# Triangle blocks of a gated delta rule solved one block per partition, and no modulation sums during a norm

## The chip, the cores and the metric

The kernel runs on one core of one Trainium2 chip. The metric is the device time of one execution in microseconds (us), lower is better; the time of a kernel is the median of several executions.

## What is computed

One decoder layer with adaLN conditioning: 256 tokens, width 2048, all in float32. A vector `mod` is made from the conditioning vector, then follow a SwiGLU feed-forward (FFN1, inner width 5632), a token mixer with 8 softmax-attention heads and 8 gated-delta-rule heads, a second feed-forward (FFN2) and a last norm.

```python
mod = cond @ ada_w[l] + ada_b[l]
sh1, sc1, gt1, sh2, sc2, gt2, sh3, sc3, gt3 = jnp.split(mod, N_MOD, axis=-1)
h = ada_in(x, norm_g[l, 0], sh1, sc1)          # rmsnorm(x) * (1 + scale) + shift
x = x + MACARON_W * gt1[:, None, :] * swiglu(h, ffn_w_gate[l, 0], ffn_w_up[l, 0], ffn_w_down[l, 0])
h = ada_in(x, norm_g[l, 1], sh2, sc2)
x = x + gt2[:, None, :] * hybrid_mixer(h, w_in[l], w_out[l], ...)
h = ada_in(x, norm_g[l, 2], sh3, sc3)
x = x + MACARON_W * gt3[:, None, :] * swiglu(h, ffn_w_gate[l, 1], ffn_w_up[l, 1], ffn_w_down[l, 1])
return rmsnorm(x, final_norm)
```

Inside the delta rule each head has four chunks of 64 tokens, and for each chunk the inverse of a lower triangle of 64x64 with ones on its diagonal is wanted:

```python
lower = jnp.where(strict, jnp.einsum("bhnid,bhnjd->bhnij", kb, k) * decay, 0.0)
t_inv = lax.linalg.triangular_solve(eye + lower, jnp.broadcast_to(eye, lower.shape),
                                    left_side=True, lower=True, unit_diagonal=True)
u = t_inv @ vb
```

## The kernel before, in words

**The weight stream.** All weights of the two feed-forwards and the mixer pass through one stream of 674 blocks. A block is eight tiles of 128x128. SP issues its load `wraw` (512 KB, L97, three buffers), ScalarE (ACT) casts it to a rounded high part `whi` (L99), VectorE (DVE) subtracts to get the low part `wlo` (L115), and TensorE (PE) multiplies with both parts. A load can only be issued when the `wlo` three blocks earlier is done with its buffer. Blocks 0 to 263 are FFN1, 264 to 377 the projections of the mixer, 378 to 409 its output projection, 410 to 673 FFN2.

**The modulation sums.** `mod` is not made at once: a side job `ada_col` (L237) loads one column group `adat` (1 MB, L256) and lets DVE multiply it with the conditioning and add it up (L258). 140 of these are left for the stream: each block adds a `pace` from the table `RATE` to `W.owed`, and each time that reaches one a sum is put in. While `W.quiet` is set nothing is added. Four finished columns of a gate go through DRAM as a row (`row_send`, gd<-mod, L284; `row_load`, gtr<-gd, L290).

**The norms.** `modulate` (L384) makes the normed and modulated input `hs` in 16 column groups j, of which `h_need` keeps four ahead of the matmuls. For each pair of j: x times the reciprocal norm (`xn`, ACT L401 and DVE L397), transposes on PE into `pxt` (L404), and per j a scale and shift and a split into high and low part (`ht`, `hs`: ACT L409, L410, L412; DVE L413, L414).

**The mixer and its chains.** While the stream's projections run, small serial work of the heads is put between their tiles. Each piece is a Python generator in a chain; `tick` (called per tile, 0.35 us by the kernel's own table) takes the next step of a chain when its due time, the yielded gap times `GAP`, has come. `finish(kind, h)` drains a chain to head h. The order of the projections is a written list, `ORDER = "K3 K4 K5 K6 K7 Z0 G0 V0 F0 G1 ..."`. In the chain "k" lie `gates`, `keys(h)` for each delta-rule head (transposes `pk` L896, products `pkk` L899, and the triangle `Ln` L909), and `solve(half)` behind the keys of heads 3 and 7.

**The solve.** Only the 16x16 blocks on the diagonal of the triangles are inverted here, 64 of them per half (8 matrices of 128 with 8 blocks each). Before, eight transfers bring the blocks of all matrices to DRAM (ld<-Ln, L922), and eight bring them back so that each block's 256 numbers stand on the 16 partitions of its rows (x<-ld, L927). Then 15 steps of a product (L934) and a sum (L935) run on 128 partitions, and L937 spreads the result `U0`, from which `gdn(h)` starts. `solve(0)` stands in "k" ahead of the keys of heads 4 to 7, and step G0 finishes "k".

**Order on an engine.** A scheduler orders the instructions within each engine; an engine runs its list in that order, and an instruction that waits holds all that stand behind it. `tc.issue_after(W.last)` puts a transfer behind the latest weight load in SP's list.

Of the kernel before, what the change touches and what calls it, by code (L numbers as in the profile page):

```python
# [16 lines left out]
P = 128  # L17
# [13 lines left out]
NH = 8  # L31
# [3 lines left out]
N_TILES = 5392  # L35
GR = 24
NEG = -1e30

RATE = ((0, 0.5), (24, 0.34), (56, 0.45), (68, 0.35), (112, 0.45), (168, 0.38), (264, 0.1), (280, 0.18), (408, 0.125))
N_BIG, N_GDN = 3, 3  # L40
# [3 lines left out]
X_LATE = {2: (2, 6), 4: (6, 11), 7: (11, 16)}  # L44
TILE_US = 0.35
MORE = True
GAP = {"k": 1.0, "gdn": 1.0, "fox": 1.2}
ORDER = ("K3 K4 K5 K6 K7 Z0 G0 V0 F0 G1 F1 G2 F2 G3 F3 V1 Z1 G4 F4 G5 F5 G6 F6 G7 F7").split()
N_O = 17
MAGIC = 0x5F3759DF  # L50
# [79 lines left out]
def layer_kernel(ctx: ExitStack, tc: tile.TileContext, xt, xrow, c, adaw, cols, cst, fng, w, out, order, dbg=None):  # L130
# [89 lines left out]
    def C(name, lo_=0, n=None):  # L220
        o, wd = CST[name]
        return cstt[:, o + lo_ : o + (wd if n is None else lo_ + n)]
# [161 lines left out]
    def modulate(which, m_sh, m_sc, hs):  # L384
        ada_need(max(m_sh, m_sc), KD - 1)
        g1 = gains(which, m_sc, 0, KD)
        y = [norm_rstd(t) for t in range(2)]
        st = {}

        def one(j):  # L390

            if j % 2 == 0:
                st["ps"] = psf("pxt")
                for t in range(2):
                    xn = tmp.tile([P, T], F32, name="xn", bufs=4)
                    if t:
                        last = V.tensor_scalar(xn, X(t, j * P, T), y[t], None, ALU.mult)  # L397
                        if j == 0:
                            W.held = [None, sqa["hold"], last.ins]
                    else:  # L400
                        A.activation(xn, X(t, j * P, T), AF.Copy, scale=y[t])  # L401
                    for q in range(2):
                        o = q * T + t * P
                        PE.transpose(st["ps"][:, o : o + P], xn[:, q * P : (q + 1) * P], ident)  # L404
            ps = st["ps"][:, (j % 2) * T : (j % 2 + 1) * T]
            g, sh = g1[:, j : j + 1], mod[:, m_sh * KD + j : m_sh * KD + j + 1]
            t = pt("ht")
            if j % 2:
                A.activation(t, ps, AF.Identity, bias=sh, scale=g)  # L409
                A.copy(hs[:, j, 0], t)  # L410
            else:
                A.activation(hs[:, j, 0], ps, AF.Identity, bias=sh, scale=g)  # L412
                V.tensor_scalar(t, ps, g, sh, ALU.mult, ALU.add)  # L413
            V.tensor_tensor(hs[:, j, 1], t, hs[:, j, 0].bitcast(F32), ALU.subtract)  # L414

        hq["next"], hq["one"] = 0, one

# [12 lines left out]


    clock = {"now": 0.0}
    chains = {"k": [], "gdn": [], "fox": []}
    due = {"k": 0.0, "gdn": 0.0, "fox": 0.0}

    def advance(kind):

# [17 lines left out]
    def start(kind, h, chain):  # L455
        if not chains[kind]:
            due[kind] = clock["now"] + GAP[kind]
        chains[kind].append((h, chain))
# [256 lines left out]
    def mixer():  # L715
# [3 lines left out]
        dram = lambda n, sh: mx.enter_context(tc.tile_pool(name=n + "p", bufs=1, space=bass.MemoryType.DRAM)).tile(sh, F32, name=n)  # L719
        xd = dram("xd", [P, KD, T])  # L720
        rows = dram("rowd", [NH, 2 * T])
        ld = dram("ld", [2 * NH, 8, 16, 16])
        op = mx.enter_context(tc.tile_pool(name="op", bufs=N_O))
        gp = mx.enter_context(tc.tile_pool(name="gp", bufs=1))
        m1p = mx.enter_context(tc.tile_pool(name="m1p", bufs=1))
# [160 lines left out]
        def keys(h):  # L886
# [20 lines left out]
            V.tensor_tensor(nb2, nbt[:, :, h], r2[:, :, h], ALU.mult)  # L907
            for t in range(2):
                V.scalar_tensor_tensor(Ln[:, h, t], pg[:, t * P : (t + 1) * P], nb2[:, t : t + 1], dec[:, t], ALU.mult, ALU.mult)  # L909

        def solve(half):

# [3 lines left out]
            V.tensor_tensor(rb2[:, :, hs4], nbeg[:, :, hs4], r2[:, :, hs4], ALU.mult)  # L916
            rk = rsqrt(ssk[:, :, hs4], [P, 2, 4], "k")
            V.tensor_tensor(rkb[:, :, hs4], rk, colS[:, :, 4, hs4], ALU.mult)
            Lh = Ln[:, hs4].rearrange("p h t j -> p (h t) j")
            for b in range(8):  # L920
                r = slice(16 * b, 16 * b + 16)
                nc.sync.dma_start(ld[ht, b].rearrange("n r c -> r n c"), Lh[r, :, r])  # L922
            rows_ = x[:, ht]
            for b in range(8):
                r = slice(16 * b, 16 * b + 16)
                src = ld[ht, b].rearrange("n r c -> n (r c)").unsqueeze(0).to_broadcast([16, n, 256])
                nc.sync.dma_start(rows_[r], src)  # L927
            yield 9.0
            U = tmp.tile([P, n, 16], F32, name="u16", bufs=1)
            pr = tmp.tile([P, n, 16], F32, name="pr16", bufs=1)  # L930
            G.memset(rows_[:, :, 0:256:17], 1.0)
            V.tensor_copy(U, C("id16").unsqueeze(1).to_broadcast([P, n, 16]))
            for i in range(1, 16):
                V.tensor_tensor(pr[:, :, : i + 1], rows_[:, :, 16 * i : 16 * i + i + 1], U[:, :, : i + 1], ALU.mult)  # L934
                V.tensor_reduce(U[:, :, i], pr[:, :, : i + 1], mybir.AxisListType.X, ALU.add)  # L935
            for q in range(2):
                V.tensor_tensor(  # L937
                    U0[:, hs4].rearrange("p h t (b i) -> p (h t) b i", b=4)[:, 4 * q : 4 * q + 4],
# [200 lines left out]
        def have_keys(h, ps):  # L1139
            kk[h] = otile("kk")  # L1140
            conv_silu(ps, NH + h, kk[h].bitcast(F32)[:, 0])
            start("k", h, keys(h))
            if h % 4 == 3:
                start("k", h, solve(h // 4))

        def step(kind, h):
            if kind == "K":
                have_keys(h, project([("qkv", NH + h)])[0])
            elif kind == "G":
                pq = project([("qkv", h)])[0]  # L1150
                pv = project([("qkv", 2 * NH + h)])[0]
                finish("gdn", h - 3)
                finish("k", h // 4 * 4 + 3)
                qv[h] = otile("qv")
                conv_silu(pq, h, qv[h].bitcast(F32)[:, 0])
                conv_silu(pv, 2 * NH + h, qv[h].bitcast(F32)[:, 1])
# [183 lines left out]
```

## Time and profile before

| | before |
|---|---|
| median of 3 runs | 2103.53 us (2102.01 to 2106.01) |
| the profiled execution's own time | 2100.51 us |
| its span in the trace | 2098.7 us |
| mean granted TensorE clock | 0.983 |
| PE busy | 2010.9 us, 96% of the span |
| DVE busy | 1484.3 us, 71% |
| ACT busy | 991.1 us, 47% |
| DMA traffic | 529.18 MB, 252 GB/s mean |

Durations in the rows are of the one profiled execution. PE is busy almost throughout, so time is lost where PE has a gap, and where the granted clock is below 1.00, since the same matmuls then take longer. A row of the waits names the instruction that was held, what released it, the sum, the number and the longest. A row of the timeline begins with the start and the duration, and ends in brackets with the idle time ahead of it and its releaser. SPq is SP's queue of transfers; a group there lasts from the first issue to the last.

### The profile page before, as it was taken

Reading aid. Unit: us, or ns where it says so; the run is one execution under the profiler, and the core shown is the slowest. Engines: PE = TensorE matmul, PEld = TensorE weight load, DVE = VectorE, ACT = ScalarE, POOL = GpSimd, SP = SyncE. Lnnn points to the kernel's source line nnn. Section 1 sums busy time; section 2 is a strip of 40 time slices with the busy share of each in tenths; the row PEclk is TensorE's granted clock in tenths of the full one; section 3 lists DMA queues with packets and bytes.
Section 4 is the critical chain, followed back from the end, with each engine's and each line's share of the span. In section 5 each row is a group of like instructions: output and inputs, shape, how many; then the busy total and the mean of one; then the engine's idle time right before and its main releaser. Section 6 shows DMA issues by size and latency. Waiting matters only on the chain. (4 is left out here: it accounts for less than half of the span.)

```text
span 2098.7 us, 25397 instructions
## 1 busy us (share of the span) xinstructions
PE 2010.9 (96%) x9347; PEld 1646.8 (78%) x9347; DVE 1484.3 (71%) x2075; ACT 991.1 (47%) x1420; POOL 2.1 (0%) x11
## 2 busy tenths in 40 slices
PE   7899999999999998789999989899999999999998
PEld 4788788777888877667888878778888888888886
DVE  6899888887877867877877876665655554445454
ACT  4544444333434446745756654553444334444443
POOL 0000000000000000000000000000000000000000
PEclk8999999999999999989999999999999999999999
DMA  9899999998888875575556557566776656555553
GB/s 375 313 336 349 337 318 309 375 365 321 335 339 340 324 274 199 160 234 191 183 202 223 195 178 258 198 231 204 274 210 239 205 191 198 191 191 191 203 195 134
DMA packets 138815, 529.18 MB, mean 252 GB/s; under 512 B 23097, under 2 KB 28217, under 8 KB 120385
## 3 DMA queue, kind: packets, MB, share of 16 engines
q1 hardware_dynamic: 138690, 527.56, 70.7%
q8 instruction: 73, 1.20, 0.2%
q14 instruction: 52, 0.43, 0.1%
HBM read 523.13 MB, written 4.37 MB: 251 GB/s over the span
## 5 line engine op out<-in xcount | busy, mean ns | idle before, releaser
L99 ACT CAST whi<-wraw 128x1024 fp32r<-128x1024 f32 x674 | 705.2, 1052 | 856.2 <-DMA wraw<-in_w_dram 352.8
L115 DVE TENSOR_TENSOR wlo<-wraw,whi 128x1024 fp32r<-128x1024 f32 x674 | 814.3, 1221 | 380.5 <-ACT whi L99 375.6
L517 PE MATMUL pgu<-whi,hs 128*128 128x512 f32 x1408 | 553.1, 395 | 11.8 <-ACT hs L370 5.9
L518 PE MATMUL pgu<-whi,hs 128*128 128x512 f32 x1408 | 550.6, 392 | 4.3 <-DVE hs L414 4.3
L520 PE MATMUL pgu<-wlo,hs 128*128 128x512 f32 x1408 | 439.0, 393 | 8.7 <-DVE wlo L115 8.3
L258 DVE CUSTOM_DVE_ANT_0 adat<-adat,cs,colt 128x2048 f32<-128x2048 f32 x140 | 328.5, 2347 | 68.4 <-DMA adat<-in_ada_dram 67.0
L517 PEld LDWEIGHTS pgu<-whi,hs 128*128 128x128 f32 x1408 | 266.9, 190 | 70.9 <-ACT hs L370 6.7
L520 PEld LDWEIGHTS pgu<-wlo,hs 128*128 128x128 f32 x1408 | 264.8, 189 | 70.1 <-DVE wlo L115 15.4
L518 PEld LDWEIGHTS pgu<-whi,hs 128*128 128x128 f32 x1408 | 266.6, 189 | 60.3 <-DVE hs L414 4.7
L517 PE MATMUL pd<-whi,hid 128*128 128x512 f32 x704 | 274.4, 390 | 1.3 <-ACT whi L99 1.3
L518 PE MATMUL pd<-whi,hid 128*128 128x512 f32 x704 | 274.0, 389 | 0.0
L461 PE MATMUL pp<-hs,whi 128*128 128x512 f32 x656 | 244.7, 408 | 8.5 <-ACT whi L99 7.0
L520 PE MATMUL pd<-wlo,hid 128*128 128x512 f32 x704 | 223.3, 390 | 3.5 <-DVE wlo L115 3.5
L462 PE MATMUL pp<-hs,wlo 128*128 128x256 f32 x656 | 190.2, 290 | 2.6 <-DVE wlo L115 2.6
L520 PEld LDWEIGHTS pd<-wlo,hid 128*128 128x128 f32 x704 | 131.8, 188 | 33.1 <-DVE wlo L115 6.0
L517 PEld LDWEIGHTS pd<-whi,hid 128*128 128x128 f32 x704 | 132.1, 188 | 29.1 <-ACT whi L99 1.7
L518 PEld LDWEIGHTS pd<-whi,hid 128*128 128x128 f32 x704 | 132.2, 188 | 27.3
L461 PEld LDWEIGHTS pp<-hs,whi 128*128 128x128 f32 x656 | 126.1, 192 | 33.8 <-ACT whi L99 7.8
L462 PEld LDWEIGHTS pp<-hs,wlo 128*128 128x128 f32 x656 | 126.7, 193 | 4.6 <-DVE wlo L115 3.7
L764 PE MATMUL pv<-whi,hs 128*128 128x512 f32 x128 | 53.0, 421 | 3.9 <-ACT whi L99 3.9
L765 PE MATMUL pv<-wlo,hs 128*128 128x512 f32 x128 | 52.8, 413 | 3.6 <-DVE wlo L115 3.6
L766 PE MATMUL pv<-whi,hs 128*128 128x512 f32 x128 | 51.8, 405 | 0.0
(304 smaller groups left out, 1347.9 us busy)
## 6 DMA issues: line engine op xcount, KB each, us to landing
wraw<-in_w_dram SPq DMA_DIRECT2D x674, 512.0 KB, 4.5
adat<-in_ada_dram SPq DMA_DIRECT2D x140, 1024.0 KB, 7.6
gtr<-gd SPq DMA_DIRECT2D x12, 256.0 KB, 6.3
rw<-rowd SPq DMA_DIRECT2D x24, 128.0 KB, 3.5
xr<-in_xr_dram SPq DMA_DIRECT2D x4, 512.0 KB, 4.6
adaf<-in_ada_dram SPq DMA_DIRECT2D x4, 512.0 KB, 9.9
adaf<-in_ada_dram SPq DMA_DIRECT2D x2, 1024.0 KB, 12.0
x<-in_xr_dram SPq DMA_DIRECT2D x4, 512.0 KB, 8.8
```

What stands on the lines that cost most here:

```text
L99: self.cast = self.nc.scalar.copy(self.h, r).ins
L115: nc.vector.tensor_tensor(self.l, r, self.h.bitcast(F32), ALU.subtract)
L258: V.tensor_tensor_reduce(t, t, cs, HALF.get(m, 1.0), L("adab", q, 1), ALU.mult, ALU.add, mod[:, q : q + 1])
L461: PE.matmul(ps, wt[0], act.rearrange("p a t -> p (a t)"), start=first, stop=False)
L462: PE.matmul(ps[:, :T], wt[1], act[:, 0], start=False, stop=last)
L517: PE.matmul(ps[t], hi_(t), wh, start=first, stop=False)
L518: PE.matmul(ps[t], lo_(t), wh, start=False, stop=False)
L520: PE.matmul(ps[t], hi_(t), wl, start=False, stop=last)
L764: PE.matmul(pv[t], hs[:, k, 0, sl], wh, start=(k == 0), stop=False)
L765: PE.matmul(pv[t], hs[:, k, 0, sl], wl, start=False, stop=False)
L766: PE.matmul(pv[t], hs[:, k, 1, sl], wh, start=False, stop=(k == KD - 1))
```

## The change

It has two parts.

**The solve** becomes a chain of its own, "s", started at the end of `keys(3)` and `keys(7)`; G0 and G4 finish it. Through DRAM it takes one transfer of the eight whole matrices (ld<-Ln, 512 KB, rows of 512 bytes) and one back that picks the diagonal blocks, one block on each of 64 partitions (x<-ld, 64x16x16: 1024 pieces of 64 bytes). The 15 steps then run on 64 partitions and solve all 16 columns at once, with twice as many elements per partition. The result goes to DRAM (xi<-x) and comes back on 128 partitions (u<-xi, again 1024 pieces of 64 bytes). Each of the four transfers is pinned behind the latest weight load, and the chain yields between them. Buffers: the block, the solution and the products lie in parts of `x`; the POOL engine clears them.

**The norms** set `W.quiet` from their start to the last j, so that no modulation sum falls into them. In both the mixer's and FFN2's norm this moves the later sums and their transfers back.

```diff
-GAP = {"k": 1.0, "gdn": 1.0, "fox": 1.2}
+GAP = {"k": 1.0, "s": 1.0, "gdn": 1.0, "fox": 1.2}
@@ modulate
         st = {}
+        W.quiet = True
...
             V.tensor_tensor(hs[:, j, 1], t, hs[:, j, 0].bitcast(F32), ALU.subtract)
+            if j == KD - 1:
+                W.quiet = False
@@ mixer
-        ld = dram("ld", [2 * NH, 8, 16, 16])
+        ld = dram("ld", [2 * NH, 8 * DIAG])
+        xi = dram("xi", [2 * NH, 8, 256])
@@ keys
+            if h % 4 == 3:
+                start("s", h, solve(h // 4))
@@ solve
-            Lh = Ln[:, hs4].rearrange("p h t j -> p (h t) j")
-            for b in range(8):
-                r = slice(16 * b, 16 * b + 16)
-                nc.sync.dma_start(ld[ht, b].rearrange("n r c -> r n c"), Lh[r, :, r])
-            rows_ = x[:, ht]
-            for b in range(8):
-                r = slice(16 * b, 16 * b + 16)
-                src = ld[ht, b].rearrange("n r c -> n (r c)").unsqueeze(0).to_broadcast([16, n, 256])
-                nc.sync.dma_start(rows_[r], src)
-            yield 9.0
+            with tc.issue_after(W.last):
+                nc.sync.dma_start(ld[ht, : P * P].rearrange("n (r c) -> r n c", c=P), Ln[:, hs4].rearrange("p h t j -> p (h t) j"))
+            yield 6.0
+            L_, X_, pr = (x[:64, 4 + i] for i in range(3))
+            src = ld[ht].rearrange("n (b q) -> (n b) q", q=DIAG)[:, : 16 * P].rearrange("m (r c) -> m r c", c=P)[:, :, :16]
+            with tc.issue_after(W.last):
+                nc.sync.dma_start(L_.rearrange("p (r c) -> p r c", c=16), src)
+            G.memset(X_, 0.0)
+            G.memset(X_[:, 0:256:17], 1.0)
+            yield 6.0
+            Xv = X_.rearrange("p (c i) -> p c i", i=16)
+            G.memset(L_[:, 0:256:17], 1.0)
+            for i in range(1, 16):
+                m = i + 1
+                pv = pr[:, : 16 * m].rearrange("p (c j) -> p c j", j=m)
+                V.tensor_tensor(pv, Xv[:, :, :m], L_[:, 16 * i : 16 * i + m].unsqueeze(1).to_broadcast([64, 16, m]), ALU.mult)
+                V.tensor_reduce(Xv[:, :, i], pv, mybir.AxisListType.X, ALU.add)
+                if i % 4 == 3:
+                    yield 1.0
+            yield 4.0
+            with tc.issue_after(W.last):
+                nc.sync.dma_start(xi[ht].rearrange("n b q -> (n b) q"), X_)
+            yield 6.0
             U = tmp.tile([P, n, 16], F32, name="u16", bufs=1)
-            pr = tmp.tile([P, n, 16], F32, name="pr16", bufs=1)
-            G.memset(rows_[:, :, 0:256:17], 1.0)
-            V.tensor_copy(U, C("id16").unsqueeze(1).to_broadcast([P, n, 16]))
-            for i in range(1, 16):
-                V.tensor_tensor(pr[:, :, : i + 1], rows_[:, :, 16 * i : 16 * i + i + 1], U[:, :, : i + 1], ALU.mult)
-                V.tensor_reduce(U[:, :, i], pr[:, :, : i + 1], mybir.AxisListType.X, ALU.add)
+            with tc.issue_after(W.last):
+                nc.sync.dma_start(U, xi[ht].rearrange("n b (c i) -> (b c) n i", i=16))
+            yield 6.0
@@ have_keys and the step G
-            if h % 4 == 3:
-                start("k", h, solve(h // 4))
...
                 finish("k", h // 4 * 4 + 3)
+                finish("s", h // 4 * 4 + 3)
```

What this does to the order on the engines is shown at three places. Line numbers of the changed kernel are a few higher (the weight load is L98 there, `wlo` L116, the sum L259).

**SP, where the triangles go to DRAM and come back.** Before, from the last rows of the decay factors (rw) that the keys need; both halves are in these rows:

```order
L850 DMA rw<-rowd 128x256 x3
L922 DMA ld<-Ln 16x8x16 x8
L927 DMA x<-ld 16x8x256 x8
L97 DMA wraw<-in_w_dram 128x1024
L256 DMA adat<-in_ada_dram 128x2048
L97 DMA wraw<-in_w_dram 128x1024
L850 DMA rw<-rowd 128x256
L97 DMA wraw<-in_w_dram 128x1024 x3
L922 DMA ld<-Ln 16x8x16 x8
L927 DMA x<-ld 16x8x256 x8
```

Now, from the second weight load ahead of the first half's transfer; the solve's transfers stand between weight loads:

```order
L98 DMA wraw<-in_w_dram 128x1024 x2
L855 DMA rw<-rowd 128x256 x2
L98 DMA wraw<-in_w_dram 128x1024
L927 DMA ld<-Ln 128x8x128
L855 DMA rw<-rowd 128x256 x2
L932 DMA x<-ld 64x16x16
L98 DMA wraw<-in_w_dram 128x1024 x3
```

And further down, the second half's way to DRAM and back (L927, L932) and the first half's results (L947, L951):

```order
L927 DMA ld<-Ln 128x8x128
L98 DMA wraw<-in_w_dram 128x1024
L855 DMA rw<-rowd 128x256
L98 DMA wraw<-in_w_dram 128x1024
L257 DMA adat<-in_ada_dram 128x2048
L98 DMA wraw<-in_w_dram 128x1024
L932 DMA x<-ld 64x16x16
L98 DMA wraw<-in_w_dram 128x1024
L947 DMA xi<-x 64x256
L98 DMA wraw<-in_w_dram 128x1024
L951 DMA u_7026<-xi 128x8x16
```

Sixteen issues in one place, with no weight load between them, have become single ones. The first half's blocks come back with only two small transfers between their way out and their way in; the second half's stand three weight loads apart, and the first half's results go out and come back one and two weight loads later.

**DVE, in the first half's steps.** The names are `pr` and `u` for products and solution before; now all three are parts of `x`. Before, in the middle of the first steps:

```order
L934 TENSOR_TENSOR pr_6780<-x,u_6779 128x8x4
L935 TENSOR_REDUCE u_6779<-pr_6780 128x8
L934 TENSOR_TENSOR pr_6780<-x,u_6779 128x8x5
L935 TENSOR_REDUCE u_6779<-pr_6780 128x8
L934 TENSOR_TENSOR pr_6780<-x,u_6779 128x8x6
L935 TENSOR_REDUCE u_6779<-pr_6780 128x8
L934 TENSOR_TENSOR pr_6780<-x,u_6779 128x8x7
L935 TENSOR_REDUCE u_6779<-pr_6780 128x8
L934 TENSOR_TENSOR pr_6780<-x,u_6779 128x8x8
L115 TENSOR_TENSOR wlo<-wraw,whi 128x1024
L935 TENSOR_REDUCE u_6779<-pr_6780 128x8
```

Now:

```order
L116 TENSOR_TENSOR wlo<-wraw,whi 128x1024
L941 TENSOR_TENSOR x<-x 64x48
L116 TENSOR_TENSOR wlo<-wraw,whi 128x1024
L942 TENSOR_REDUCE x<-x 64x16
L941 TENSOR_TENSOR x<-x 64x64
L942 TENSOR_REDUCE x<-x 64x16
L941 TENSOR_TENSOR x<-x 64x80
L942 TENSOR_REDUCE x<-x 64x16
L116 TENSOR_TENSOR wlo<-wraw,whi 128x1024
L909 TENSOR_SCALAR ssk<-ssk 128x2
L941 TENSOR_TENSOR x<-x 64x96
```

Before, the first 13 solve instructions stand between one `wlo` and the next, and 40 rows hold the whole half; now one to four stand between two `wlo`, together with work of the keys.

**DVE, at the end of FFN2's norm.** Before, behind `hs` of the 12th to 14th column group:

```order
L414 TENSOR_TENSOR hs<-ht,hs 128x256
L413 TENSOR_SCALAR ht<-pxt,g_11316,mod 128x256
L414 TENSOR_TENSOR hs<-ht,hs 128x256
L115 TENSOR_TENSOR wlo<-wraw,whi 128x1024
L414 TENSOR_TENSOR hs<-ht,hs 128x256
L258 ISA adat,mod<-adat,cs,colt 128x2048
L258 ISA mod 128x1
L413 TENSOR_SCALAR ht<-pxt,g_11316,mod 128x256
L115 TENSOR_TENSOR wlo<-wraw,whi 128x1024
L414 TENSOR_TENSOR hs<-ht,hs 128x256
```

Now, behind the 10th to 12th:

```order
L399 TENSOR_SCALAR xn<-x,nstd 128x256
L415 TENSOR_SCALAR ht<-pxt,g_11293,mod 128x256
L416 TENSOR_TENSOR hs<-ht,hs 128x256
L116 TENSOR_TENSOR wlo<-wraw,whi 128x1024
L416 TENSOR_TENSOR hs<-ht,hs 128x256
L259 ISA adat,mod<-adat,cs,colt 128x2048
L259 ISA mod 128x1
L415 TENSOR_SCALAR ht<-pxt,g_11293,mod 128x256
L116 TENSOR_TENSOR wlo<-wraw,whi 128x1024
L416 TENSOR_TENSOR hs<-ht,hs 128x256 x2
```

A sum stands in the last rows of the norm in both; it has moved up by two column groups and one `wlo`, and its load stands one weight load earlier on SP (behind wraw 423 instead of 424, counted from 0). The other sum of this norm before (ahead of `wlo` 415) is gone, as is that of the mixer's norm.

More of the change, by code (lines that the diff above doesn't have):

```diff
@@ L37 @@
 NEG = -1e30
+DIAG = 16 * P + 16
 RATE = ((0, 0.5), (24, 0.34), (56, 0.45), (68, 0.35), (112, 0.45), (168, 0.38), (264, 0.1), (280, 0.18), (408, 0.125))
@@ L432, in layer_kernel @@
     clock = {"now": 0.0}
-    chains = {"k": [], "gdn": [], "fox": []}
-    due = {"k": 0.0, "gdn": 0.0, "fox": 0.0}
+    chains = {"k": [], "s": [], "gdn": [], "fox": []}
+    due = {"k": 0.0, "s": 0.0, "gdn": 0.0, "fox": 0.0}
     def advance(kind):
```

## The prediction

> **What bounds the kernel now.** I read the first page, then the waits of PE in the stretch of the solve, then that stretch in windows of 5 us, and the queue of SP there; after that the two norms.
>
> ```profile
> PE 2010.9 (96%) x9347; PEld 1646.8 (78%) x9347; DVE 1484.3 (71%) x2075; ACT 991.1 (47%) x1420; POOL 2.1 (0%) x11
> PE   7899999999999998789999989899999999999998
> ```
>
> PE carries the time. Each digit is 52.5 us; apart from the ends the only run of low ones is slices 16 to 18 (787 to 944 us), the norm and first projections of the mixer. A gain must come from PE's gaps or from its granted clock. The waits of PE from 855 to 930 us:
>
> ```profile
> PE pp L461 <- ACT whi L99: 6.0, 1, 6.0
> PE pv L764 <- ACT whi L99: 3.9, 1, 3.9
> PE pv L765 <- DVE wlo L115: 3.6, 4, 2.0
> PE pp L462 <- DVE wlo L115: 1.7, 1, 1.7
> ```
>
> PE starves for weights twice, 6.0 + 1.7 and 3.9 + 2.0 (of the third row its longest) = 13.6 us. Windows (length; busy time and count of PE, PEld, DVE, ACT, POOL; granted clock, DMA share, GB/s) show where, and that the clock drops behind it:
>
> ```profile
> 880.00:885.00 5.00, 1.22 (x2) 0.50 (x2) 4.08 (x26) 1.04 (x1) 0.31 (x1) 0.70 0.98 374
> 885.00:890.00 5.00, 3.13 (x7) 2.51 (x8) 4.65 (x10) 1.05 (x1) 0.00 (x0) 0.50 0.70 258
> 890.00:895.00 5.00, 5.00 (x18) 3.93 (x17) 5.00 (x14) 2.58 (x4) 0.00 (x0) 0.78 0.39 110
> 900.00:905.00 5.00, 3.68 (x24) 3.17 (x22) 0.58 (x2) 1.09 (x3) 0.00 (x0) 1.00 1.14 137
> 905.00:910.00 5.00, 0.30 (x1) 0.29 (x1) 1.69 (x9) 1.04 (x1) 0.31 (x1) 0.59 1.02 351
> 910.00:915.00 5.00, 3.31 (x10) 2.42 (x10) 4.76 (x11) 1.04 (x1) 0.00 (x0) 0.50 0.82 299
> 915.00:920.00 5.00, 5.00 (x27) 4.20 (x26) 4.43 (x12) 2.67 (x4) 0.00 (x0) 0.89 0.32 105
> ```
>
> Busy time at a lower clock is lost by its missing share: 1.22 x 0.30 + 3.13 x 0.50 + 5.00 x 0.22 + 0.30 x 0.41 + 3.31 x 0.50 + 5.00 x 0.11 = 5.4 us. What starves PE stands in SP's queue and in the transfers issued between 860 and 915 us:
>
> ```profile
> 867.43 3.65 SPq L922 DMA_DIRECT2D ld<-Ln  x8
> 871.12 3.85 SPq L927 DMA_DIRECT2D x<-ld  x8
> 892.67 3.64 SPq L922 DMA_DIRECT2D ld<-Ln  x8
> 896.41 3.70 SPq L927 DMA_DIRECT2D x<-ld  x8
> wraw<-in_w_dram SPq DMA_DIRECT2D x10, 512.0 KB, 8.8
> x<-ld SPq DMA_DIRECT2D x16, 128.0 KB, 6.2
> ld<-Ln SPq DMA_DIRECT2D x16, 8.0 KB, 1.5
> ```
>
> Twice 7.5 us of issues let no weight load through, and the next ones then share the engines with 8 x 128 KB of broadcast: DMA share over 1 at 137 GB/s from 900 us. The weights land late, and both starvations follow. So solve and its transfers cost 13.6 + 5.4 = **19.0 us**.
>
> **The change, part by part.** *The solve's transfers.* The sixteen issues at one place go: a load of weights waits behind single issues now, and the traffic back falls from 1 MB of broadcast to 64 KB of blocks. With them both starvations go and their clock loss: -19.0. What is new are four transfers per half with a wait each: x<-ld for ld<-Ln, xi<-x for the last DVE step, u<-xi for xi. Each waits at the head of SP's queue, and weight loads stand behind it; SP's wait already there is the measure:
>
> ```profile
> SPq L97 <- DVE wlo L115: 1250.1, 576, 11.5
> ```
>
> That is 2.17 us a weight load that SP spends waiting for a buffer: a hold below it is free. A hold is the landing of the transfer ahead, at least 1.5 us (ld<-Ln) and at most 8.8 (a weight load in this crowd). Six holds (two x<-ld, two xi, two u) at 1.5 cost nothing, at 8.8 some 6 x 6.6 = 40 us. I stand near the lower row, since the pieces of 64 bytes are those of the old ld<-Ln and all eight of its transfers (1024 pieces) were issued in 3.65 us: half of the holds pass the slack by 2 us, **+3.0**. The first x<-ld also holds DVE, whose first step stands ahead of a `wlo`; three raw buffers of 8 x 0.35 us cover that wait.
>
> *DVE's work.*
>
> ```profile
> 882.42 0.18 DVE L934 TENSOR_TENSOR pr<-x,u 128x16 f32<-128x16 f32 x1 [0.23 <-DMA wraw<-in_w_dram]
> 897.91 0.29 DVE L934 TENSOR_TENSOR pr<-x,u 128x128 f32<-128x128 f32 x1
> ```
>
> 0.11 us for 112 elements: 0.98 ns each. The 15 steps read 8 x (2+...+16) = 1080 elements each for product and sum, now 16 x 135 = 2160: 2 x 1080 x 0.98 ns = 2.1 us more per half, 4.2 in all. DVE was busy 5.00 us of a window only where it caught up with late weights (890 to 895), so half of it is hidden: **+2.1** (0 to 4.2). That the steps now stand between `wlo` instead of ahead of them removes the first `wlo`'s delay, which is within the 19.0. Keys 4 to 7 no longer wait behind the solve; gdn(0) starts some five weight blocks later, but F0 and G1 have other work for PE: nothing. Sum for the solve: -19.0 + 3.0 + 2.1 = **-13.9**.
>
> *FFN2's norm.* Rows of DVE, PE and SP, and two windows:
>
> ```profile
> 1358.62 2.35 DVE L258 CUSTOM_DVE_ANT_0 adat<-adat,cs,colt 128x2048 f32<-128x2048 f32 x1 [8.10 <-DMA adat<-in_ada_dram]
> 1362.62 0.73 PE L520 MATMUL pgu<-wlo,hs 128*128 128x512 f32 x2 [1.67 <-DVE wlo L115]
> 1372.46 0.43 SPq L256 DMA_DIRECT2D adat<-in_ada_dram  x1
> 1380.92 2.35 DVE L258 CUSTOM_DVE_ANT_0 adat<-adat,cs,colt 128x2048 f32<-128x2048 f32 x1 [3.50 <-DMA adat<-in_ada_dram]
> 1385.27 1.22 PE L518 MATMUL pgu<-whi,hs 128*128 128x512 f32 x2 [4.33 <-DVE hs L414]
> 1380.00:1385.00 5.00, 0.94 (x5) 0.44 (x3) 4.08 (x5) 1.22 (x2) 0.00 (x0) 0.88 0.32 129
> 1385.00:1390.00 5.00, 4.73 (x11) 3.77 (x12) 1.77 (x3) 0.64 (x3) 0.00 (x0) 0.50 0.58 206
> ```
>
> Two sums each hold DVE for their load, and PE behind: 1.67 us, then 4.33 and 0.94 x 0.12 + 4.73 x 0.50 = 2.5 of clock. The first sum is gone: -1.7. The second is not: in the new order a sum still stands ahead of the norm's last rows, two column groups earlier, its load one weight load earlier. From its issue to its landing were 1380.92 - 1372.46 = 8.5 us, and between the `wlo` that frees its place on SP and the sum stands still a single `wlo`. So the wait comes again, for a column group that PE needs that much earlier: 4.3 + 2.5 stay. Together **-1.7**; if DVE, without its 8.1 us, comes late enough to the sum, up to -8.5; if the stall grows by a sum's own 2.35 us, +0.7.
>
> *The mixer's norm* had one sum, and the same chain behind it:
>
> ```profile
> 809.32 2.35 DVE L258 CUSTOM_DVE_ANT_0 adat<-adat,cs,colt 128x2048 f32<-128x2048 f32 x1 [2.11 <-DMA adat<-in_ada_dram]
> 812.79 0.66 PE L404 MATMUL pxt<-colt,xn 128*128 128x128 f32 x4 [1.98 <-ACT ht L409]
> 813.66 0.75 PE L461 MATMUL pp<-hs,whi 128*128 128x512 f32 x1 [0.21 <-DVE hs L414]
> 810.00:815.00 5.00, 2.81 (x13) 2.02 (x13) 5.00 (x8) 2.82 (x6) 0.00 (x0) 0.87 0.34 128
> 815.00:820.00 5.00, 5.00 (x25) 4.40 (x24) 2.81 (x6) 2.23 (x5) 0.00 (x0) 0.79 0.47 165
> 816.00:817.00 1.00, 1.00 (x5) 0.81 (x5) 0.97 (x3) 0.00 (x0) 0.00 (x0) 0.50 0.49 115
> ```
>
> 1.98 + 0.21 idle and 2.81 x 0.13 + 5.00 x 0.21 = 1.4 of clock: 3.6 us, and here no sum is left in the norm. The next one comes some six blocks later, its load behind four rows of the gate (gtr), so it may wait as long; nothing of a norm stands behind it: between 0 and 3.6, I take 1.6. **-2.0**.
>
> The clock was 0.50 a few us after a wait of only 1.98 us. The Trainium skill (TensorE: Matmul & The Clock Gate, What's actually happening) has the clock halved only after a whole idle window of about 3.4 us. By that rule this place would have lost 2.2 us and not 3.6; the trace does not agree, and the sum goes by the trace.
>
> *The tail of the mixer.* The sums are put off, and one more now stands in the serial chain of the last delta-rule head, between the state `st` and `vz`, where before
>
> ```profile
> 1246.37 0.35 DVE L1059 SCALAR_TENSOR_TENSOR st<-st,rw,pst 128x128 f32<-128x128 f32 x1 [0.47 <-PE pst L1054]
> 1247.30 0.29 DVE L1048 TENSOR_TENSOR vz<-u,po 64x128 f32<-64x128 f32 x1
> L258 DVE CUSTOM_DVE_ANT_0 adat<-adat,cs,colt 128x2048 f32<-128x2048 f32 x140 | 328.5, 2347 | 68.4 <-DMA adat<-in_ada_dram 67.0
> ```
>
> only 0.6 us lay between: **+2.4** for the sum (0 if its place is beside other work, 4.9 with a wait as long again). The other sums are the same number in other places, at nothing: DVE is idle 29% of the span.
>
> **Sum:** -13.9 - 1.7 - 2.0 + 2.4 = -15.2, against the profiled execution's own 2100.51: 2085.3. The median of the runs is 2103.53, 3.0 above that execution, so I forecast 2088.3.
>
> **The rivals.**
> *All of it comes.* Holds and DVE's work are hidden, both norms lose their stalls: -19.0 - 8.5 - 3.6 = -31.1, 2072.4. For it: PE waits for nothing else in these stretches. Against: the sum that is left in FFN2's norm.
> *The solve stays the bound.* The holds and the steps strewn between `wlo` starve PE much as the issues did, and only 4 of the 19.0 come: -4 - 1.7 - 2.0 + 2.4 = -5.3, 2098.2. For it: from 890 to 895 us DVE was busy without a gap; its list is still in order, and each of its waits for a transfer holds a `wlo`. Against: 0.58 and 1.69 of 5 us in the windows from 900 to 910.
> *Slower: small pieces land late.*
>
> ```profile
> gd<-mod SPq DMA_DIRECT2D x12, 2.0 KB, 10.5
> ```
>
> This transfer of 512 pieces took 10.5 us to land. If the price is per piece, x<-ld and u<-xi with 1024 pieces take 21 us, 15 more than the old x<-ld. The first step of DVE and U0 wait for them with a `wlo` right behind; the buffers' 8.4 us, less the 2.17 that SP waits anyway, cover some 6 of the 15, four transfers x 9 us = 36, 2088.3 + 36 = 2124. It decides from about 16 us to land, where four waits of 3.8 us eat the 15.2. Against it stands the row of ld<-Ln with 128 such pieces in 1.5 us.
>
> The Trainium skill (DMA: Bandwidth & Descriptors, Specifications) speaks for this one: below 512 bytes a transfer misses the line rate, and is done as read and write of more. No row here shows its price for 64 bytes beyond that of ld<-Ln, so it stays with the chance that the rows give.
>
> **How the numbers follow.** The forecast, 2079 to 2094: 0.55. All of it, 2070 to 2079: 0.17. The solve stays, 2094 to 2103: 0.17. Slower: 0.11. The range 2073 to 2103 leaves out a third of the second and the fourth: about 0.17. A measurement of this kernel can tell some 0.2%, 4.2 us, from no change: faster is below 2099.3. Faster: 0.55 + 0.17 + most of the third, 0.10 = 0.82; the same 0.08; slower 0.10.
>
> **What would show it.** Right: from the first ld<-Ln to the second half's U0, windows of 5 us in which PE is busy over 4.5 us at a clock of 1.00 and the DMA share is mostly below 1; landings of x<-ld and u<-xi under 8 us; PE's 1.67 gone, and a wait of 3 to 6 us for `hs` in FFN2's norm; the mixer's norm without a drop of the clock; a `vz` 2.4 us later in the last head. Wrong: SP's rows of xi and u held for over 5 us with PE waiting for `whi` behind them, DVE waiting over 8 us ahead of its first step or U0, or FFN2's norm without a stall, in which case the time is some 7 us lower.

## The result, and the profile after

| | before | changed |
|---|---|---|
| median | 2102.77 us (2101.69 to 2106.01, 4 runs) | 2080.80 us (2078.07 to 2085.53, 4 runs) |
| ratio to before | | 0.9895 (95% interval 0.9872 to 0.9919) |
| span of the profiled execution | 2098.7 us | 2076.3 us |

The change saves 22 us. The forecast was 15.2 us (2088.3 us for the median, 7.5 us more than measured). The first page of the changed kernel, the lines of busy time and of PE's slices:

```profile
PE 2002.4 (96%) x9347; PEld 1642.5 (79%) x9347; DVE 1486.7 (72%) x2073; ACT 989.7 (48%) x1418; POOL 2.7 (0%) x15
PE   7899999999999998999999989999999999999997
```

Of the run of low slices at 787 to 944 us one is left. All waits of PE from 855 to 930 us:

```profile
PE pv L770 <- DVE wlo L116: 1.9, 2, 1.3
PE pkk L904 <- ACT kk L908: 0.4, 1, 0.4
```

These are 2.3 us, where the same view of before sums to 18.0 (the prediction shows four of its six rows). Both waits on `whi` are gone. The windows there:

```profile
865.00:870.00 5.00, 3.67 (x18) 2.73 (x17) 4.93 (x20) 4.99 (x11) 0.12 (x1) 1.00 0.90 194
870.00:875.00 5.00, 4.48 (x21) 3.16 (x21) 4.90 (x12) 4.77 (x9) 0.00 (x0) 1.00 0.55 160
875.00:880.00 5.00, 5.00 (x24) 4.08 (x23) 4.78 (x19) 2.16 (x7) 0.00 (x0) 1.00 1.01 418
900.00:905.00 5.00, 4.92 (x24) 3.93 (x25) 4.94 (x12) 4.03 (x7) 0.00 (x0) 1.00 0.70 212
905.00:910.00 5.00, 5.00 (x33) 4.29 (x32) 4.39 (x12) 1.94 (x6) 0.00 (x0) 1.00 0.77 286
```

The clock is 1.00 throughout, and DVE is the engine that is now nearly full (4.4 to 4.9 of 5 us) beside PE. The solve's transfers on SP, and their landings over the whole kernel:

```profile
888.43 0.33 SPq L98 DMA_DIRECT2D wraw<-in_w_dram  x1
893.69 0.60 SPq L932 DMA_DIRECT2D x<-ld  x1
894.38 0.61 SPq L98 DMA_DIRECT2D wraw<-in_w_dram  x1
895.13 0.50 SPq L947 DMA_DIRECT2D xi<-x  x1
895.73 0.54 SPq L98 DMA_DIRECT2D wraw<-in_w_dram  x1
898.41 0.38 SPq L951 DMA_DIRECT2D u<-xi  x1
gd<-mod SPq DMA_DIRECT2D x12, 2.0 KB, 9.9
x<-ld SPq DMA_DIRECT2D x2, 64.0 KB, 2.8
xi<-x SPq DMA_DIRECT2D x2, 64.0 KB, 3.3
u<-xi SPq DMA_DIRECT2D x2, 64.0 KB, 4.5
```

The landings are medians of those in the trace: x<-ld has one (2.8 us), u<-xi two (2.7 and 6.3). Weight loads slip in between the transfers; the longest the queue is held is about 5 us (888.76 to 893.69), by x<-ld of the second half, which waits for the first half's steps and their buffer.

**Where the time went, by stage.** Every kernel here runs the same 5392 matmuls that read `whi`, in the same order, so the start of the same matmul can be compared between two traces. The table gives how much longer (+) or shorter each stage is than before, in us; stages are named by the times of before. One execution stands behind each row, and equal code does not repeat exactly: FFN1 (20 to 782 us), which no kernel here alters, came out between -2.6 and +3.9, and in the solve's stage, where changed, gd_early and tail_gd run the same instructions, it was -20.8, -16.1 and -20.4. Differences under 5 us in that stage decide nothing below.

| profiled execution of | norm 782-833 | solve 833-945 | 945-998 | mixer 998-1224 | tail 1224-1256 | FFN2's norm and behind 1344-1426 | to the end |
|---|---|---|---|---|---|---|---|
| changed | -3.9 | -20.8 | +1.8 | -0.8 | +2.8 | -1.8 | +0.2 |
| quiet_only | -4.7 | -1.8 | -0.4 | -0.7 | +4.4 | -1.2 | -2.3 |
| solve_only | 0.0 | -14.0 | -1.6 | -0.4 | +4.4 | -2.4 | +2.2 |
| old_in_chain | -4.4 | -4.5 | -1.0 | -3.6 | +4.8 | -4.6 | +1.5 |
| new_in_keys | -3.5 | -18.3 | +1.4 | -3.3 | +6.4 | -5.1 | +0.3 |
| old_spread | -3.5 | +16.4 | -0.7 | -2.5 | +6.7 | -4.8 | -1.1 |
| new_burst | -3.9 | -8.4 | +1.0 | -1.1 | +4.3 | -1.6 | -1.5 |
| new_traffic | -4.4 | -11.3 | +1.2 | -2.2 | +4.2 | -1.5 | -2.0 |
| steps_at_once | -4.6 | -21.3 | -1.6 | -1.4 | +2.8 | -5.2 | -1.6 |
| holds_twice | -4.4 | -21.8 | +6.9 | -3.0 | +3.3 | -1.4 | -1.4 |
| gd_early | -3.9 | -16.1 | +0.8 | -1.3 | +2.8 | -6.0 | -2.6 |
| tail_gd | -4.6 | -20.4 | +3.3 | -2.5 | +1.8 | -7.9 | -2.6 |
| all_three | -4.2 | -20.6 | 0.0 | -1.4 | +4.5 | -8.0 | -2.7 |

### The profile page after: what moved, and what is told of

It is laid out like the page before. It is cut to its first block, busy times and chain, and to the rows that moved or that the text cites. A ratio compares the mean times of both kernels' runs of the same rounds, so it can differ in the third digit from the quotient of the medians.

```text
span 2076.3 us, 25353 instructions
## 1 busy us (share of the span) xinstructions
PE 2002.4 (96%) x9347; PEld 1642.5 (79%) x9347; DVE 1486.7 (72%) x2073; ACT 989.7 (48%) x1418; POOL 2.7 (0%) x15
## 4 chain that ended last, share of the span: by engine, by line
PE 79%; DVE 8%; DMA 7%; ACT 3%; issue 2%; SPq 0%; ACTq 0%; DVEq 0%
PE pgu L524 13%; PE pgu L521 13%; PE pgu L522 13%; PE pd L524 7%; PE pd L522 7%; PE pd L521 7%; DMA wraw<-in_w_dram 5%; PE pp L465 4%; DVE wlo L116 4%; PE pp L466 2%; PE po L521 1%; PE po L522 1%; PE po L524 1%; ACT whi L100 1%; DVE adat L259 1%
## 5 line engine op out<-in xcount | busy, mean ns | idle before, releaser
L116 DVE TENSOR_TENSOR wlo<-wraw,whi 128x1024 fp32r<-128x1024 f32 x674 | 814.8, 1222 | 376.3 <-ACT whi L100 372.8
L259 DVE CUSTOM_DVE_ANT_0 adat<-adat,cs,colt 128x2048 f32<-128x2048 f32 x140 | 328.7, 2348 | 62.5 <-DMA adat<-in_ada_dram 61.5
```

Of the source, the lines that this page charges most:

```text
L116: nc.vector.tensor_tensor(self.l, r, self.h.bitcast(F32), ALU.subtract)
L259: V.tensor_tensor_reduce(t, t, cs, HALF.get(m, 1.0), L("adab", q, 1), ALU.mult, ALU.add, mod[:, q : q + 1])
```

## The experiments

**The two parts apart.** quiet_only sets `W.quiet` in the kernel before; solve_only takes it out of the changed one.

```diff
@@ quiet_only, against before, in modulate
+        W.quiet = True
...
+            if j == KD - 1:
+                W.quiet = False
```

> The kernel before with only W.quiet set during the two norms; the solve as before. If the parts add up as the trace of the changed kernel shows them (mixer's norm -2.5, tail of the mixer +2.7, FFN2's norm and what follows it -2), this is within 4 us of the kernel before, and both starvations of PE in the solve (6.0 and 3.9 us on whi) are still there. If the norms are what paid, it is 10 us or more faster.

> The changed kernel without W.quiet in the norms; the solve as changed. If the solve carries the gain: 18 to 23 us faster than before, in the projections of the mixer alone, with the stalls of both norms as before (1.98 us on ht, 4.33 us on hs). If the norms paid, under 12 us.

quiet_only: 2091.78 us, ratio 0.9950 (0.9934 to 0.9965). solve_only: 2088.50, 0.9939 (0.9920 to 0.9959). The two add up to the whole (0.5% + 0.6% against 1.05%), but both expectations were missed: by the medians the norms alone pay 10 us, the solve alone 14. The stalls of both norms were expected in solve_only as before: the mixer's is there (1.98 us on `ht`), but in FFN2's norm PE waits 3.16 us on `wlo` and 0.54 on `hs`, where before it waited 1.67 and 4.33. The table says part of it. The norm of the mixer gains 3.5 to 4.7 in every kernel that has the quiet and nothing in solve_only; PE's starvations in quiet_only's solve are as before (6.1 and 5.3 us on `whi`). And solve_only's stage gains 14 where the kernels with both parts gain 16 to 22: without the quiet norms the decays (rw) and the triangles come in one piece on SP, and no weight load goes out from 857.7 to 871.2 us:

```profile
857.70 0.33 SPq L98 DMA_DIRECT2D wraw<-in_w_dram  x1
859.46 4.48 SPq L852 DMA_DIRECT2D rw<-rowd  x3
864.81 0.38 SPq L924 DMA_DIRECT2D ld<-Ln  x1
865.29 0.52 SPq L852 DMA_DIRECT2D rw<-rowd  x1
868.34 0.70 SPq L929 DMA_DIRECT2D x<-ld  x1
871.19 0.35 SPq L98 DMA_DIRECT2D wraw<-in_w_dram  x1
```

In the changed kernel one more weight load stands among these rows, ahead of ld<-Ln (the order in the section on the change), and no stretch there is longer than 7 us. So in this trace some of the solve's gain comes only with both parts; how much is not shown, since the medians add up without it. Of quiet_only's 10 us, 4.7 are the norm's; its profiled execution gained 8 in all, and the rest lies in small amounts before and behind, no more than equal code varies, so where it comes from stays open.

**Transfers or place.** old_in_chain gives the old solve a chain of its own; new_in_keys puts the new one back behind the keys.

```diff
@@ old_in_chain, against quiet_only          (new_in_keys: the reverse, against the changed kernel)
-            if h % 4 == 3:
-                start("k", h, solve(h // 4))
@@ keys
+            if h % 4 == 3:
+                start("s", h, solve(h // 4))
```

> quiet_only plus the old solve (sixteen transfers in one place, 15 steps on 128 partitions) moved into a chain of its own, started by keys(3) and keys(7). Theory 1, the burst of sixteen issues with 1 MB of broadcast starves PE of weights: the gain of the chain alone is small, PE waits again 3 us or more for whi behind each x<-ld group, the clock drops to 0.50, and the time stays within 8 us of the kernel before. Theory 2, it was the place in the chain of the keys (keys 4 to 7 queue behind the solve, whose DVE steps stand in one piece): 14 us or more faster, as the changed kernel.

> The changed kernel with its new solve back in the chain of the keys, started behind keys(3) and keys(7) as before. Theory 1 (the transfers): 14 us or more of the 22 stay. Theory 2 (the place): under 8 us stay. In both, the stretch of the solve reaches further, since keys 4 to 7 wait for a longer chain and G0 has to drain it; up to 6 us may go there.

old_in_chain: 0.9948 (0.9930 to 0.9966), the same as quiet_only. Its waits of PE in the solve are still these:

```profile
PE pv L767 <- ACT whi L99: 4.4, 1, 4.4
PE pp L464 <- ACT whi L99: 3.6, 1, 3.6
```

new_in_keys: 2078.18 us, 0.9882 (0.9856 to 0.9909), no slower than the changed kernel. The chain of its own is worth nothing that can be told in the medians, and 2.5 and 2.7 us of the stage, which is inside its spread; the transfers carry it, issues and traffic together. The second theory falls.

**Issues, traffic, or both.** new_burst adds issues without traffic, new_traffic the traffic in one issue, and old_spread spreads the old issues out.

```diff
@@ new_burst, behind x<-ld
+            for e in range(14):
+                o = 16 * (e % 8)
+                with tc.issue_after(W.last):
+                    nc.sync.dma_start(x[o : o + 16, 7, P * (e // 8) : P * (e // 8) + P], ld[n * half + e % 8, : 16 * P].rearrange("(r c) -> r c", c=P))
@@ new_traffic, behind x<-ld
+            with tc.issue_after(W.last):
+                nc.sync.dma_start(x[:, 8:16], ld[ht, :256].unsqueeze(0).to_broadcast([P, n, 256]))
@@ old_spread, against old_in_chain: each ld<-Ln and x<-ld
+                with tc.issue_after(W.last):
+                    ...
+                yield 0.7            (1.4 for x<-ld)
```

> The changed kernel with 14 loads of 8 KB that nobody uses issued in one piece behind x<-ld in each half (into a part of x that holds nothing then): 14 x 0.46 = 6.4 us of SP's queue per half, but only 112 KB of traffic. If the burst of issues starves PE: the stretch of the solve (-20.8 in the changed kernel) loses 6 us or more, with PE waiting for whi behind the burst and the clock falling. If it is the broadcast's traffic: it loses under 3 us.

> The changed kernel with one more transfer per half beside x<-ld: 1 MB broadcast to 128 partitions in a single issue (into x[:, 8:16], which holds nothing then; the value is not used), the traffic of the old way back without its issues. new_burst, the issues without the traffic, lost 12.4 of the 20.8 us of the solve's stretch. If the burst of issues is the whole cause, this one loses under 3 us; if the rest of it is the broadcast's traffic, it loses about 8 (6 to 12), with DMA shares over 1 at under 160 GB/s and weight loads that land in over 8 us there.

> old_in_chain with its sixteen transfers per half pinned behind weight loads and 0.7 to 1.4 tile-times of 1 us apart in the chain; on SP the second half's then stand one to four between weight loads, the first half's still nearly together. The 1 MB of broadcast per half stays. If the burst of issues on SP starves PE: the second half's wait on whi (3.6 us in old_in_chain, at about 905 us) goes, and the stretch from the last projection ahead of the solve to 945 us of before gains 6 us or more over old_in_chain (-4.5). If the broadcast's traffic does it, the stretch stays within 3 us of old_in_chain and the DMA share is over 1 at under 160 GB/s there.

new_burst: 2091.90, 0.9929 (0.9913 to 0.9946): the solve's stage loses 12.4 us of its 20.8 to issues of 8 KB. The queue of its second half:

```profile
891.53 0.33 SPq L98 DMA_DIRECT2D wraw<-in_w_dram  x1
893.37 0.48 SPq L951 DMA_DIRECT2D xi<-x  x1
893.90 0.58 SPq L257 DMA_DIRECT2D adat<-in_ada_dram  x1
895.32 0.38 SPq L955 DMA_DIRECT2D u<-xi  x1
895.81 0.62 SPq L932 DMA_DIRECT2D x<-ld  x1
896.48 8.83 SPq L936 DMA_DIRECT2D x<-ld  x14
905.40 12.10 SPq L98 DMA_DIRECT2D wraw<-in_w_dram  x6
910.00:915.00 5.00, 3.33 (x11) 2.26 (x11) 3.51 (x8) 3.10 (x4) 0.00 (x0) 0.50 0.20 78
```

No weight load goes out for 13.9 us, and the last row, a window behind it, shows PE at 3.33 of 5 us and at half the clock, as before, though the DMA share is 0.20. So issues without traffic cost time. The wait on `whi` that was expected is small, though: 1.1 us behind the first half's burst, where the kernel loses 3.7 us against the changed one. Behind the second, where it loses 10.6, PE has no matmul of the weights from 903.3 to 912.2 us and does the serial work of step G0 in one piece, which waits for other engines, this row the longest:

```profile
906.38 0.33 PE L983 MATMUL pvq<-colt,qv 128*128 128x128 f32 x1 [2.50 <-ACT qv L887]
```

In the changed kernel the same work stands between matmuls of the weights.

new_traffic: 2085.19, 0.9921 (0.9896 to 0.9946), the stage 9.5 us worse than the changed kernel's. By its expectation the rest of the cause would be traffic, but the trace says otherwise for part of it:

```profile
889.55 0.33 SPq L98 DMA_DIRECT2D wraw<-in_w_dram  x1
889.93 1.76 SPq L257 DMA_DIRECT2D adat<-in_ada_dram  x1
891.75 0.44 SPq L934 DMA_DIRECT2D x<-ld  x1
899.84 0.60 SPq L932 DMA_DIRECT2D x<-ld  x1
901.21 1.05 SPq L98 DMA_DIRECT2D wraw<-in_w_dram  x2
```

In the second half x<-ld (L932) stands one weight load further up than in the changed kernel and waits 7.6 us at the head of SP's queue for the first half's last steps, whose buffer it shares; again no weight load for 11.7 us. Only the first half, with an order as in the changed kernel, shows traffic by itself: PE busy 7.43 of the 10 us from 870 to 880 against 9.48, some 2 us. The median landing of a weight load from 855 to 935 us is 4.7 us, but the three right behind that broadcast take 7.1 in the median, against 3.4 at the same place of the changed kernel.

old_spread: 1.0002 (0.9987 to 1.0018), 16 us worse in the stage. It could not tell what it was made for: the transfers moved apart on SP, but the first half's stayed nearly together, and the longer chain ran into step G0, which waited for it (PE 5.0 us on `qv`). What it shows is that spreading sixteen transfers in this way did not make them cheap.

One reading puts part of this together: the stretches in which SP issues no weight load. Of the 833 to 945 us stage, all such stretches of over 8 us in each trace:

| kernel | stretches without a weight load, us | solve's stage |
|---|---|---|
| steps_at_once, holds_twice, changed | 9.7; 9.2; 9.2 | -21.3; -21.8; -20.8 |
| new_in_keys | 10.1 | -18.3 |
| solve_only | 9.1, 13.5 | -14.0 |
| new_traffic | 9.2, 11.7 | -11.3 |
| new_burst | 9.2, 12.7, 13.9 | -8.4 |
| old_in_chain | 9.3, 10.4, 16.2, 9.5 | -4.5 |
| quiet_only | 9.4, 11.8, 16.3, 9.3 | -1.8 |
| before | 9.1, 14.5, 8.2, 8.4 | 0 |
| old_spread | 10.3, 10.7, 10.7, 12.1, 8.7, 12.6 | +16.4 |

The first, of 9 to 11, is common to all; gd_early, tail_gd and all_three have that one alone. Among the kernels with the new transfers, each further one of 11 us or more goes with 6 to 10 us, whether issues fill the queue or a waiting transfer holds it. With the old transfers the reading is not enough: old_in_chain, before and old_spread lose 16, 21 and 37 us against the changed kernel with one, one and two such stretches. The second starvation of before (3.9 us on `whi`) follows stretches of 8.2 and 8.4 us only, shorter than the one that all kernels have, and costs 10.8 us against the changed kernel, the first 8.6. The three weight loads issued behind its broadcasts, from 900 to 905 us, landed in 9.2 us in the median. So the traffic has a part in it, as the prediction said; how much is issues and how much traffic the runs do not divide.

**The steps, and the holds.**

```diff
@@ steps_at_once, in solve
-                if i % 4 == 3:
-                    yield 1.0
@@ holds_twice, in solve: xi<-x, and likewise u<-xi
-                nc.sync.dma_start(...)
+                for _ in range(2):
+                    nc.sync.dma_start(...)
```

> The changed kernel without the yields between its 15 steps, so that the program has them in one piece. If strewn steps matter, PE waits for wlo behind them and the stretch of the solve loses 3 us or more; by the transfers' theory it stays within 2 us of the changed kernel's -20.8, since 30 small instructions are under 10 us of DVE and three weight blocks lie ready.

> The changed kernel with xi<-x and u<-xi each sent twice, the second time waiting for the first to land: four more holds at the head of SP's queue in all, each of a landing of 3 to 5 us by the changed kernel's rows. By the step of the prediction (half of the holds pass SP's slack by 2 us) the stretch of the solve loses about 4 us. By the trace of the changed kernel, where weight loads behind xi and u came in time, it loses under 1.5 us.

steps_at_once: 2078.18, 0.9860 (0.9836 to 0.9884), -21.3 in the stage; strewing the steps is worth nothing that can be told. holds_twice: 2081.81, 0.9891 (0.9869 to 0.9913). The stage is untouched (-21.8), but the next one is 5.1 us worse than in the changed kernel, and the worst of all: the second half's u<-xi comes late, DVE stands before U0 for 1.76 us, and behind it PE waits 3.35 us for the attention chain. The four holds cost 4 us in all (-21.8 + 6.9 against -20.8 + 1.8); the medians differ by 1.0 us, so the size is that of one execution. The way is not the prediction's: it goes through DVE's list and not through SP's queue and the weights. The changed kernel shows the same way, in one row of DVE and one of PE:

```profile
938.90 0.76 DVE L954 TENSOR_TENSOR U<-u,cstt 128x256 f32<-128x256 f32 x2 [2.84 <-DMA u<-xi]
940.85 0.39 PE L466 MATMUL pp<-hs,wlo 128*128 128x256 f32 x1 [1.80 <-DVE wlo L116]
```

**The sum behind gd, and the sum in the tail.** In the changed kernel the stall of FFN2's norm is not where the prediction left it. DVE, SP, PE and two windows:

```profile
1350.46 2.34 DVE L259 CUSTOM_DVE_ANT_0 adat<-adat,cs,colt 128x2048 f32<-128x2048 f32 x1
1362.60 0.43 SPq L285 DMA_DIRECT2D gd<-mod  x1
1368.03 0.43 SPq L257 DMA_DIRECT2D adat<-in_ada_dram  x1
1381.48 2.35 DVE L259 CUSTOM_DVE_ANT_0 adat<-adat,cs,colt 128x2048 f32<-128x2048 f32 x1 [8.40 <-DMA adat<-in_ada_dram]
1386.23 1.11 PE L543 MATMUL pz<-colt,sg 128*128 128x128 f32 x4 [4.17 <-DVE sg L575]
1365.00:1370.00 5.00, 5.00 (x24) 4.14 (x23) 2.62 (x3) 2.11 (x2) 0.00 (x0) 1.00 1.00 22
1385.00:1390.00 5.00, 3.77 (x11) 3.19 (x12) 5.00 (x6) 0.65 (x2) 0.00 (x0) 0.50 0.64 199
```

The sum inside the norm no longer waits. The next one does, 30 us further, and its load stands behind gd<-mod: 2 KB in 512 pieces of 4 bytes, during which the DMA engines are busy (1.00) at 22 GB/s. gd_early moves gd away from the load; tail_gd also keeps the sums out of the last head; all_three adds steps_at_once.

```diff
@@ gd_early, in row_soon
-        for n in ROW_LAG:
+        for n in (3, 13) if m == 8 else ROW_LAG:
@@ tail_gd, besides, in step and ahead of x_back
             elif kind == "G":
+                W.quiet = h == 7
...
+        W.quiet = False
```

> The changed kernel with gd<-mod of FFN2's gate sent 3 blocks behind its last sum instead of 6, so that the next load of a sum is five weight loads behind it and not two. If the load behind those 512 pieces of 4 bytes makes the new stall behind FFN2's norm (PE 4.17 us on sg, a sum 8.40 us on its load), that wait of the sum is under 1 us and the stretch from FFN2's norm on (-1.8) gains another 4 to 6.5 us. If it is only the sum's place, the stall stays.

> gd_early with W.quiet also from step G7 to the end of the mixer's projections, so that no sum stands in the last delta-rule head. By the trace that sum costs 2.3 us (PE's wait on vz): the stretch at the tail (+2.75) falls to between 0 and 0.5, and the whole is 2 to 3 us faster than gd_early. If the sums moved back meet another stall, it shows in the output projection or FFN2's norm.

> tail_gd and steps_at_once together. If the gains add: 2 to 3 (tail) + 4 to 6.5 (gd) below the changed kernel's 2080.8, and up to 2 for the steps in one piece: 2068 to 2075, ratio to before 0.982 to 0.987.

gd_early: 2076.09, 0.9865 (0.9840 to 0.9891). The stage is at -6.0. With gd in its old place it was -1.8 in the changed kernel and between -1.2 and -5.2 in the others, since the stall's length varies (PE 4.17 us on `sg` in the changed kernel, 1.6 in steps_at_once), so what the move is worth lies between 1 and 5 us. The sum's wait falls by more than half, though not under 1 us:

```profile
1383.50 2.35 DVE L259 CUSTOM_DVE_ANT_0 adat<-adat,cs,colt 128x2048 f32<-128x2048 f32 x1 [3.87 <-DMA adat<-in_ada_dram]
```

PE's wait on `sg` is 0.80. tail_gd: 2072.13, 0.9862 (0.9839 to 0.9884). In the tail it was expected to bring 2 to 3 us, and brought 1.0 (+2.8 to +1.8), given back in the output projection (+1.8), where PE now waits 1.3 us on `wlo`. The wait on `vz` is gone, as this row of the changed kernel is, but the windows of tail_gd there show the clock down all the same:

```profile
1225.36 0.69 PE L1067 MATMUL po<-vz,At 128*64 128x128 f32 x2 [2.29 <-DVE vz L1065]
```

```profile
1215.00:1220.00 5.00, 3.95 (x19) 3.14 (x19) 2.73 (x9) 1.61 (x6) 0.00 (x0) 0.70 0.66 202
1225.00:1230.00 5.00, 3.79 (x12) 2.79 (x13) 3.73 (x21) 1.43 (x6) 0.00 (x0) 0.72 0.44 158
```

That is 3.95 x 0.30 + 3.79 x 0.28 = 2.2 us of clock, in a stretch of short gaps that before passed at 1.00. solve_only shows the same without any change to the sums: its sum stands where it stood before, PE waits on `vz` for 0.8 us as before, and yet the tail is 4.4 us longer, at this clock:

```profile
1220.00:1225.00 5.00, 3.95 (x16) 3.00 (x15) 2.29 (x10) 1.61 (x6) 0.00 (x0) 0.58 0.64 210
1225.00:1230.00 5.00, 4.63 (x18) 3.37 (x16) 1.50 (x8) 1.10 (x5) 0.00 (x0) 0.50 0.03 6
```

So the clock decides much of this stage, with the sum or without it. In the changed kernel it was at 0.87 and 0.50 from 1220 to 1230 us. Why it falls there was not tried further. all_three: 2069.72, 0.9845 (0.9827 to 0.9863), the fastest of all, its interval just below the changed kernel's (from 0.9872). The time is as expected, the sum behind it is not: the tail brought nothing there (+4.5). By the table most of the difference is in FFN2's stage (-8.0 against -1.8): with the sums put off, gd goes out some 27 us later (in tail_gd at 1389.39 against 1362.60), away from the norm and from the sum behind it.

## Why the prediction was right, point by point

- **The solve's transfers starve the weights (-19.0): right in mechanism, too small in size.** The waits of PE fell from 18.0 to 2.3, 15.7 us, and 5.4 of clock came back: 21.1, close to the stage's 20.8. The prediction counted only 13.6 of the 18.0; it left out the smaller ones in the same stretch (`pk` on Ln 1.9, 1.6 more of `pv` on `wlo`, `pkk` 0.9). That the old transfers as a whole starve PE is shown (old_in_chain, new_in_keys); what issues and broadcast each cost is not.
- **The holds (+3.0): near in size, by luck.** Half of six holds at 2 us each are 6.0 and not 3.0, so the term did not follow from its own words; with 6.0 the forecast would have been 2091.3. And SP's queue is not where they cost: PE waits for no `whi` from 855 to 930 us. What cost time is that DVE waits 2.84 us for u<-xi ahead of the second half's U0, and PE 1.80 for the `wlo` behind it, which fits the +1.8 of the stage behind. In gd_early and tail_gd, with the same instructions there, that wait of DVE is 1.20 and 3.02 us and the stage at +0.8 and +3.3.
- **DVE's work (+2.1): mis-sized.** It is not seen as a loss: DVE is busy up to 5.00 of 5 us in the stage, but PE's waits on `wlo` from 855 to 930 us are 1.9, where before they were 3.6 and 1.7. Solve in all: -13.9 forecast, -20.8 + 1.8 = -19.0 measured. This is 5 of the 7 us by which the forecast was short, and no more than this stage varies.
- **The mixer's norm (-2.0): -3.9.** The stall went as said (3.6); the 1.6 for the next sum, behind the gate's rows, was not paid: that sum waited 0.98 us for its load.
- **FFN2's norm (-1.7): the size is right (-1.8) by luck, its reason is not.** The prediction kept 4.3 + 2.5 for the sum left in the norm. That sum came free of any wait, its load being issued 6.2 us ahead of it and landing in 5.6. The norm itself gained 8.4 us (up to 1410 us of before), so -8.5 was the right bound there. In its place a new stall of 6.5 us stands behind the norm, at the load that goes out behind gd<-mod, which the prediction did not see; gd_early, with gd moved, has 2.2 there, but steps_at_once, with gd in its old place, 3.0, so how much of it is gd's is not shown. The prediction's sign for this case, a time some 7 us lower than forecast, came true in its number (7.5), but not for this reason, since the stall had only moved.
- **The tail (+2.4): +2.8**, and its row (2.29 on `vz`) as forecast. But solve_only, without that wait, lost 4.4, and taking the sum away brought back 1.0 in tail_gd and nothing in all_three. So the step is right about the wait and not about what it is worth; the clock, which this term did not count, has a part in the size, and the agreement is luck.
- **The rivals.** All of it comes: it did, and a little more (-20.8, -3.9 and -8.4 are -33.1 against -31.1), but the new stall behind the norm, the tail and the wait for u<-xi took 11.1 back. The forecast had counted all three in about this size, the stall for another reason and the holds by another way, so that the time fell into its range is luck in part. Small pieces land late: they land in 2.7 to 6.3 us, far from the 16 at which it would decide. The solve stays the bound: no; but solve_only and new_burst show what it would have looked like. That the two parts do not act on each other was assumed and not said; solve_only's extra stretch without weight loads shows that one changes SP's order for the other.

## What to carry to other kernels

In a kernel that lives on a stream of loads through one queue, look for the longest stretch in which that queue issues none of them: here every kernel passed one of 9 to 11 us, and with the new transfers each further one of over 11 cost 6 to 10, whether 14 issues of 0.46 us or a transfer that waits at the head filled it. Look at the landings behind it as well, since the old broadcasts starved PE behind a stretch of 8.4. Count what a helper job shifts, too: moving the sums out of the norms changed which transfers stood together on SP some 50 us later. And a stall that is removed should be looked for at the next place with the same neighbours; here it was again a load behind gd<-mod: before, gd<-mod went out at 1341.80 us, and the load for which DVE waits 8.10 us at 1344.07.

## What the runs showed of the hardware that was not expected

- Pieces of 64 bytes were cheap and pieces of 4 bytes were not: 64 KB in 1024 pieces of 64 bytes, read from DRAM, landed in 2.7 to 6.3 us, 2 KB in 512 pieces of 4 bytes, written to DRAM, in 9.9 in the median, with the DMA engines at a share of 1.00 and 22 GB/s meanwhile, and the 1 MB load behind it in 13.4 us instead of 7.4 in the median. The landings of the changed kernel from 1362 to 1384 us, and the median over the whole of it:

```profile
adat<-in_ada_dram SPq DMA_DIRECT2D x1, 1024.0 KB, 13.4
gd<-mod SPq DMA_DIRECT2D x1, 2.0 KB, 9.7
adat<-in_ada_dram SPq DMA_DIRECT2D x140, 1024.0 KB, 7.4
```

- The granted clock fell behind gaps of PE of 2 us and less: to 0.50 in the mixer's norm before (a gap of 1.98), to 0.70 and 0.72 as means of 5 us in the tail of tail_gd (1.84 the longest). The Trainium skill (TensorE: Matmul & The Clock Gate, What's actually happening) has a whole idle window of about 3.4 us for that; these runs do not agree.
